# Six of the second branch's gate blocks as seven block products a pair, with closer substitutions and a later chain for the new tokens

## The chip, the cores and the metric

The kernel runs on one core of a Trainium2 chip. The metric is the device time of one execution in microseconds (us). About 0.5% of it, 6 us, is what a measurement of this kernel can tell from no change.

The engines are named as the profile names them: PE (TensorE, matmuls), PEld (its weight loads), DVE (VectorE), ACT (ScalarE), POOL (GpSimd) and SP (SyncE, which here issues most DMAs).

## The reference, cut to what matters

One decoder layer works on 512 prompt positions and 8 new tokens, 520 columns in all, with a model width of 1024. A first SwiGLU block, a token mixer and a second SwiGLU block follow each other, each between two RMS norms. The mixer has two branches, retention and gated delta, of four heads each, and merges them by two sigmoid gates of 1024 channels each:

```python
proj = (h @ w_in).astype(f32)
rq, rk, rv, rg, conv_in, gz, ga, gb, gate_r, gate_g = jnp.split(proj, idx, axis=-1)
...
cq, s_conv_new = short_conv(conv_in, s_conv.astype(f32), gdn_conv_w.astype(f32))
gq = gq * lax.rsqrt(jnp.sum(gq * gq, axis=-1, keepdims=True) + EPS) * (GDN_DK ** -0.5)
gk = gk * lax.rsqrt(jnp.sum(gk * gk, axis=-1, keepdims=True) + EPS)
...
a_mat = jnp.eye(c, dtype=jnp.float32) + jnp.where(strict, bc[..., :, None] * dm * kk, 0.0)
u_v = lax.linalg.triangular_solve(a_mat, bc[..., None] * vc, left_side=True, lower=True, unit_diagonal=True)
...
y = (jax.nn.sigmoid(gate_r) * (o_r @ w_ret_branch) + jax.nn.sigmoid(gate_g) * (o_g @ w_gdn_branch))
y = (y @ w_out).astype(h.dtype)
```

The triangular systems have 64 rows, one for each chunk of 64 positions and head. The change bears on `gate_g` (how the product `h @ w_in` is formed for it), on when the triangular systems are solved, and on when the new tokens' part of the delta branch runs. What is computed stays the same.

## The kernel before, in words

All matrices are fp32. To keep the accuracy, an operand is split into a rounded part (`whi`, `xhl`'s first half) and a rest (`wlo`, its second half), and a product is three passes, lines 422 to 424: high by high, low by high, high by low. A unit of weights is a block of 1024 x 128 numbers. It is loaded by SP as `raw` (line 288 for the mixer's input weights), split by ACT (`whi`, line 360) and DVE (`wlo`, line 361), and multiplied with the 520 columns in two halves of 260: 8 contraction blocks x 3 passes x 2 halves = 48 matmuls.

Where two units belong together, the kernel can form them as seven block products instead of eight (the Strassen-Winograd scheme, table `SEVEN`). The two SwiGLU blocks do so for their gate and up weights. A pair then takes 7 x 12 = 84 matmuls in place of 96. For that it needs sums of quarters of the weights: `begin_pair` (line 292) loads three quarters by SP (`s3`, `s1`, `a22`), and `add_sums` (line 305) adds two further quarters to them by DMAs that accumulate, issued by POOL (line 308) six ticks later. `split_seven` (line 363) makes the operands `w` out of them on ACT (line 378) and DVE (line 379), and adds the remaining sums on DVE. It needs factors of the other side too (`T1` to `T4`), made from x by `token_factors` (line 747), and `product7` (line 779) issues the matmuls.

The order of the work is written out by a clock of ticks. `product` calls `tick` (line 224) after each six matmuls. A tick issues what is due among the spawned tasks, which are generators: each yields the number of ticks after which it wants to go on, and the table `LATER` shifts single steps of single tasks. So what stands in each engine's queue is fixed when the program is built, and each engine goes through its queue in order. `prefetch` (line 313) loads and splits units ahead of their use.

The mixer (line 1038) goes through the units of `w_in` in the order of `proj_order`: decay inputs, the delta branch's k, q and v of four heads, the retention branch's q, k and v, then the two output gates of the heads (`RG` and `GZ`), then eight units of the first merge gate (`GR`) and eight of the second (`GG`). After each two merge-gate units stands one unit of branch weights, whose products `br` (48 matmuls for two output blocks) take the heads' outputs `oh` and `ol` as their operands. `branch` (line 1136) merges them on DVE (line 1154) and POOL (line 1155).

With each head's v the task `gdn_head` (line 1376) is spawned. It forms `rr`, the normalisation of q and k, by a small power on POOL (line 1394), and from it `cols` on DVE (line 1403). Then `inverse` (line 1492) inverts the unit triangular matrices `AT`: blocks of 32 are laid out through DRAM (`s1`, then `L`), 31 steps of two POOL instructions each (lines 1521 and 1522, on the tile `pack`) do the substitution, eight DMAs write the result to DRAM (line 1527), four read it back turned (line 1530), DVE transposes it (line 1537), and PE uses it, in `pV` first (line 1547). `TURN` = 48 is the least distance in ticks between two heads' substitutions, and the substitution's own 31 steps are spread over 39 ticks.

With the last v of the delta branch the task `decode_gdn` (line 1711) is spawned for the new tokens. It sends out two states by POOL, convolves on DVE (`dcv`, lines 1722 and 1724), takes a silu on ACT, squares on DVE (`gsq`, line 1728), and PE sums the squares in `cs` (line 1615, in `rsqrt`).

`finish_decode` (line 1769) writes the new tokens' columns into `oh` and `ol`, ahead of the first `br` of each branch; the main loop calls it itself.

## Time and profile before

| | before |
|---|---|
| median of 3 runs | 1226.57 us (1226.17 to 1230.27) |
| the profiled execution's own time | 1229.19 us |
| its span | 1227.4 us |
| mean granted PE clock | 0.983 |
| matmuls | 9921 |
| PE busy | 1192.2 us (97%) |
| DVE busy | 898.7 us (73%) |
| ACT busy | 575.0 us (47%) |
| POOL busy | 278.4 us (23%) |
| moved by DMA | 170.36 MB |

The page gives each engine's busy time, then the chain of work that ended last, then groups of instructions by line. "out<-in" names the tile that an instruction writes and those that it reads; a bracket such as [2.30 <-POOL rr L1394] says how long the engine stood idle before it and what ended that. The lines of a helper stand for all who call it: 422 to 424 are the matmuls of every product. Matmuls overlap, so the duration of one (some 280 ns) is longer than its pitch.

### The profile page before, as it was taken

To read this page: it belongs to the slowest core of one execution; us is meant where nothing else is said; L and a number is where in the kernel's file an instruction comes from. 1 tells how busy PE (TensorE), PEld (TensorE's weight loads), DVE (VectorE), ACT (ScalarE), POOL (GpSimd) and SP (SyncE) were. 2 spreads that over 40 slices of the span, in tenths; PEclk is the share of its full clock that TensorE was granted. 3 is DMA by queue.
4 is the path that set the end of the run, shared out by engine and by line. 5 is a ranking of instruction groups with operands and counts; after the bars stand their busy time and mean duration, and the time that the engine had idled before them with its cause. 6 is when DMAs were issued, how large, how long until landed. Compare 5 with 4: busy or idle time off the path is not lost.

```text
span 1227.4 us, 25453 instructions
## 1 busy us (share of the span) xinstructions
PE 1192.2 (97%) x9921; PEld 1179.4 (96%) x9921; DVE 898.7 (73%) x1932; ACT 575.0 (47%) x1197; POOL 278.4 (23%) x501
## 2 busy tenths in 40 slices
PE   8999999999999998999999999999999999999995
PEld 7999999999998998999999999999999999999994
DVE  8988888776547887767676666547888888867554
ACT  6655666553325664322333343324565666653330
POOL 4211111000014148545541112213311111000003
PEclk8999999999998999999999999999999999999997
DMA  6887776223351433332435454342587777332352
GB/s 195 217 196 193 188 178 159 63 81 95 95 178 60 166 106 95 108 102 83 132 102 166 164 200 138 125 164 69 162 233 189 186 177 187 93 93 80 96 167 70
DMA packets 79688, 170.36 MB, mean 139 GB/s; under 512 B 17232, under 2 KB 20144, under 8 KB 79568
## 3 DMA queue, kind: packets, MB, share of 16 engines
q1 hardware_dynamic: 67280, 144.46, 37.0%
q0 software_dynamic: 12288, 24.29, 11.2%
q8 instruction: 77, 1.26, 0.4%
q14 instruction: 43, 0.35, 0.1%
HBM read 156.88 MB, written 11.83 MB: 137 GB/s over the span
## 4 chain that ended last, share of the span: by engine, by line
PE 79%; DVE 9%; ACT 4%; POOL 2%; issue 2%; DMA 2%; SPq 0%; ACTq 0%; DVEq 0%; POOLq 0%
PE sv L423 10%; PE sv L422 10%; PE sv L424 10%; PE p L422 6%; PE dn L422 6%; PE dn L424 6%; PE dn L423 6%; PE p L423 6%; PE p L424 6%; DVE wlo L361 2%; PE br L422 1%; PE br L423 1%; PE br L424 1%; PE g L423 1%; PE g L424 1%
## 5 line engine op out<-in xcount | busy, mean ns | idle before, releaser
L422 PE MATMUL p<-xhl,whi 128*128 128x260 f32 x768 | 227.7, 296 | 0.0
L424 PE MATMUL p<-xhl,wlo 128*128 128x260 f32 x768 | 218.4, 284 | 1.4 <-DVE wlo L361 1.4
L423 PE MATMUL p<-xhl,whi 128*128 128x260 f32 x768 | 218.9, 285 | 0.0
L361 DVE TENSOR_TENSOR wlo<-raw,whi 128x1024 fp32r<-128x1024 f32 (+2 forms) x120 | 139.6, 1170 | 43.2 <-ACT whi L360 41.5
L422 PE MATMUL sv<-th,w 128*128 128x260 f32 x592 | 167.4, 283 | 0.5 <-ACT q L848 0.5
L423 PE MATMUL sv<-tl,w 128*128 128x260 f32 x592 | 167.7, 283 | 0.0
L424 PE MATMUL sv<-th,w 128*128 128x260 f32 x592 | 167.3, 283 | 0.0
L424 PEld LDWEIGHTS p<-xhl,wlo 128*128 128x128 f32 x768 | 146.7, 191 | 1.6 <-DVE wlo L361 1.6
L422 PEld LDWEIGHTS p<-xhl,whi 128*128 128x128 f32 x768 | 146.7, 191 | 1.0
L423 PEld LDWEIGHTS p<-xhl,whi 128*128 128x128 f32 x768 | 147.0, 191 | 0.0
L379 DVE TENSOR_TENSOR w<-s,w 128x512 fp32r<-128x512 f32 x148 | 101.7, 689 | 38.8 <-ACT w L378 37.7
L308 POOL DMA_DIRECT2D s<-gu_in x74 | 65.1, 977 | 284.8 <-DMA s<-gu_in 143.1
L424 PE MATMUL dn<-hh,wlo 128*128 128x260 f32 x448 | 126.7, 283 | 1.2 <-DVE wlo L361 1.2
L360 ACT CAST whi<-raw 128x1024 fp32r<-128x1024 f32 (+2 forms) x120 | 115.4, 970 | 26.4 <-DMA raw<-dn_in 16.8
L422 PE MATMUL dn<-hh,whi 128*128 128x260 f32 x448 | 126.9, 283 | 0.0
L423 PE MATMUL dn<-hl,whi 128*128 128x260 f32 x448 | 126.6, 282 | 0.0
L423 PE MATMUL sv<-xhl,w 128*128 128x260 f32 x444 | 125.6, 283 | 0.0
L424 PE MATMUL sv<-xhl,w 128*128 128x260 f32 x444 | 125.4, 283 | 0.0
L422 PE MATMUL sv<-xhl,w 128*128 128x260 f32 x444 | 125.3, 282 | 0.0
L422 PEld LDWEIGHTS sv<-th,w 128*128 128x128 f32 x592 | 111.5, 188 | 0.8 <-ACT q L848 0.7
L424 PEld LDWEIGHTS sv<-th,w 128*128 128x128 f32 x592 | 111.7, 189 | 0.0
L423 PEld LDWEIGHTS sv<-tl,w 128*128 128x128 f32 x592 | 111.2, 188 | 0.0
(412 smaller groups left out, 3249.7 us busy)
## 6 DMA issues: line engine op xcount, KB each, us to landing
raw<-gu_in SPq DMA_DIRECT2D x50, 512.0 KB, 5.2
raw<-win_in SPq DMA_DIRECT2D x48, 512.0 KB, 3.7
s<-gu_in SPq DMA_DIRECT2D x74, 256.0 KB, 5.7
s<-gu_in POOLq DMA_DIRECT2D x74, 256.0 KB, 5.2
raw<-dn_in SPq DMA_DIRECT2D x32, 448.0 KB, 3.5
a<-gu_in SPq DMA_DIRECT2D x37, 256.0 KB, 6.1
x<-x SPq DMA_DIRECT2D x32, 260.0 KB, 5.3
raw<-dn_in SPq DMA_DIRECT2D x16, 512.0 KB, 3.7
```

Source lines behind the costliest of these rows:

```text
L308: self.nc.gpsimd.dma_start(out=out, in_=term, accum_op=ALU.add)
L360: self.nc.scalar.copy(hi[:, ks], t[:, ks])
L361: self.nc.vector.tensor_tensor(lo[:, ks], t[:, ks], hi[:, ks].bitcast(F32), ALU.subtract)
L379: nc.vector.tensor_tensor(w[:, 1], t[i], w[:, 0].bitcast(F32), ALU.subtract)
L422: mm(ps, hi[:, k, :], xh, start=first, stop=False, skip_group_check=more)
L423: mm(ps, hi[:, k, :], xl, start=False, stop=False, skip_group_check=more)
L424: mm(ps, lo[:, k, :], xh, start=False, stop=last, skip_group_check=more)
```

## The change

The last six of the eight `GG` units become three pairs of seven products each (`PLAIN_GATES` = 2 units stay plain). `begin_pair` and `load_to` take `win` as a source. The factors `T1` to `T4` are made in a new task, `gate_factors`, which runs beside the `GR` gates: it waits 40 ticks, and then four times reads four pieces of x back from DRAM (260 KB for each two blocks and half) and calls `factors`, which is the body of the old `token_factors`, twice. A new function, `gate_pair`, issues the products and writes the two gates. While `GG` runs, `prefetch` splits at most one unit for each tick (`most`).

The distance between two heads' substitutions goes from 48 to 40 ticks, and a substitution's steps take one more tick at each eighth step and not at each fourth, 35 ticks in all. In `decode_gdn` the wait of 20 ticks at the start becomes 28, and the one of 6 ahead of `cs` gets 2 more. `finish_decode` becomes a task spawned ahead of the `GR` units, with its instructions grouped by engine; the main loop ticks on until it is done.

```diff
-TURN = 48
+TURN = 40
+FACTORS = (40, 10, 6)
...
-    ("decode_gdn", 0): {10: 3},
+    ("decode_gdn", 0): {1: 8, 2: 2, 10: 3},
...
             for i in range(n, n + 2 * KD, 2):
-                out += [("win", i, 0, 8), ("win", i + 1, 0, 8), ("wbr", (i - n) // 2, 0, 8)]
+                if i < n + KD + PLAIN_GATES:
+                    out += [("win", i, 0, 8), ("win", i + 1, 0, 8)]
+                else:
+                    out += [("seven", "win", i, z) for z in GATE_ORDER]
+                out.append(("wbr", (i - n) // 2, 0, 8))
...
+PLAIN_GATES = 2
+GATE_ORDER = (0, 1, 2, 3, 5, 4, 6)
...
-                s1, s3, a22 = self.begun.pop((u[1], m), None) or self.begin_pair(u[1], m)
+                s1, s3, a22 = self.begun.pop(u[1:3], None) or self.begin_pair(u[1], u[2])
...
-            ahead += j > 0 and not seven and self.unit_list[j - 1][0] == "down7"
+            ahead += j > 0 and not seven and self.unit_list[j - 1][0] in ("seven", "down7")
...
+    def gate_factors(self, x_from, xs, gcol, F, first):
+
+        yield FACTORS[0]
+        for k0 in range(0, KH, 2):
+            x = [[self.slot("x", (P, 2, HC)) for _ in range(2)] for _ in range(2)]
+            for z in range(2):
+                for hf in range(2):
+                    k1 = k0 + z * KH
+                    self.nc.sync.dma_start(out=x[z][hf], in_=x_from[:, hf, k1 : k1 + 2])
+            yield FACTORS[1]
+            for k in (k0, k0 + 1):
+                yield from self.factors(k, [x[z][hf][:, k - k0] for z in range(2) for hf in range(2)], xs, gcol, F)
+                yield FACTORS[2]
+        self.begun["win", first] = self.begin_pair("win", first)
...
+        def heads(out):
+            while not ready(out):
+                yield 0
+            yield from self.finish_decode(out)
+            done.add(out)
+
+        self.spawn(heads(RG))
+        self.spawn(heads(GZ))
...
-                project(g, m)
-                project(g, m + 1)
-                if m == 0:
-                    while any((out, h) not in self.oparts for h in range(H)) or out not in self.dec_done:
-                        self.tick()
-                    self.finish_decode(out)
-                    ox = [[self.ohl[out, h, hf] for h in range(H)] for hf in range(2)]
+                if g == GR or m < PLAIN_GATES:
+                    project(g, m)
+                    project(g, m + 1)
+                else:
+                    gate[g, m], gate[g, m + 1] = self.gate_pair(F, r, first + m - PLAIN_GATES + 2 if m + 2 < KD else None, None)
+                while out not in done:
+                    self.tick()
+                ox = [[self.ohl[out, h, hf] for h in range(H)] for hf in range(2)]
...
+    def gate_pair(self, F, r, after, between):
...
+        if after is not None:
+            self.begun["win", after] = self.begin_pair("win", after)
+        for i in GATE_ORDER:
+            self.product7(SEVEN, F, "sv", banks, i)
+            a, b, c = banks
+            if i in (0, 1, 2, 5):
+                v[i] = self.work("q" if i == 1 else "u", HC)
+                nc.scalar.copy(v[i], c if i == 1 else a)
...
+            if i in (3, 4, 5):
+                t = self.work("t", HC)
+                x, y, op = ((c, 2, ALU.subtract), (b, 0, ALU.add), (v.get(1), 5, ALU.subtract))[i - 3]
+                tt(t, x, v[y], op)
+                scaled(*((1, 0), (0, 0), (1, 1))[i - 3], t)
...
-            yield 1 + (j % 4 == 0)
+            yield 1 + (j % 8 == 0)
```

How this moves the queues is seen at three places. The first is POOL's queue at the end of head 0's substitution (the tile `pack`; `rr` is the normalisation that head 3's `cols` wait for, `L` the triangular blocks). Before:

```order
L1521 TENSOR_TENSOR pack_5880<-L_5877,pack_5880 128x4x3
L1522 TENSOR_TENSOR pack_5880<-pack_5880 128x4x3
L1394 TENSOR_TENSOR rr_6538<-se_6536,mhalf 128x8
L1304 COPY rdec<-rp_6540 128x8
L1521 TENSOR_TENSOR pack_5880<-L_5877,pack_5880 128x4x2
L1522 TENSOR_TENSOR pack_5880<-pack_5880 128x4x2
L1521 TENSOR_TENSOR pack_5880<-L_5877,pack_5880 128x4
L1522 TENSOR_TENSOR pack_5880<-pack_5880 128x4
```

In the changed kernel the same place reads:

```order
L1612 TENSOR_TENSOR pack_5880<-L_5877,pack_5880 128x4x3
L1613 TENSOR_TENSOR pack_5880<-pack_5880 128x4x3
L1612 TENSOR_TENSOR pack_5880<-L_5877,pack_5880 128x4x2
L1613 TENSOR_TENSOR pack_5880<-pack_5880 128x4x2
L1612 TENSOR_TENSOR pack_5880<-L_5877,pack_5880 128x4
L1613 TENSOR_TENSOR pack_5880<-pack_5880 128x4
L1623 MEMSET TT_6547 128x512
L1626 MEMSET pack_1107_6549 64x256
L1485 TENSOR_TENSOR rr_6559<-se_6557,mhalf 128x8
L1395 COPY rdec<-rp_6561 128x8
L1612 TENSOR_TENSOR pack_6390<-L_6386,pack_6390 128x31
```

The `rr` and the `rdec` behind it have moved from within the substitution to behind its last step, ahead of head 1's first.

The second place is PE's queue where the new tokens' sums (`cs`) and head 0's first use of its inverse (`pV`) stand among the projections `p`. Before, `cs` is the 3789th matmul:

```order
L423 MATMUL p_6659<-xhl_5181,whi_6416 128x260
L424 MATMUL p_6659<-xhl_5181,wlo_6417 128x260
L1615 MATMUL cs_6679<-ones,gsq_6628 64x1
L422 MATMUL p_6658<-xhl_5040,whi_6416 128x260
L423 MATMUL p_6658<-xhl_5040,whi_6416 128x260
```

Some 80 matmuls further on, as the 3869th, comes `pV` (a row with x4 holds four matmuls):

```order
L423 MATMUL p_6752<-xhl_5232,whi_6552 128x260
L424 MATMUL p_6752<-xhl_5232,wlo_6553 128x260
L1547 MATMUL pV_6825<-pack_5880,AT_5805 32x32 x4
L1547 MATMUL pV_6826<-pack_5880,AT_5805 32x32 x4
L422 MATMUL p_6751<-xhl_5070,whi_6552 128x260
```

In the changed kernel `pV` comes first, as the 3835th matmul, and head 2's `gbc` stands right behind it:

```order
L436 MATMUL p_6757<-xhl_5168,whi_6573 128x260
L437 MATMUL p_6757<-xhl_5168,wlo_6574 128x260
L1638 MATMUL pV_6773<-pack_5880,AT_5805 32x32 x4
L1638 MATMUL pV_6774<-pack_5880,AT_5805 32x32 x4
L1339 MATMUL gbc_6793<-cst,gg 128x128 x4
L435 MATMUL p_6756<-xhl_5009,whi_6573 128x260
```

And `cs` comes behind it, as the 3869th:

```order
L436 MATMUL p_6757<-xhl_5207,whi_6573 128x260
L437 MATMUL p_6757<-xhl_5207,wlo_6574 128x260
L1706 MATMUL cs_6841<-ones,gsq_6706 64x1
L1260 MATMUL tr_6848<-cst,rv_6643 128x128 x4
L435 MATMUL p_6756<-xhl_5062,whi_6573 128x260
```

The two have changed places: `pV` has moved 34 matmuls ahead and `cs` 80 back.

The third place is POOL's queue where the `GG` gates begin (`srets_out` and `sgdns_out` are the new tokens' states, `t` is the merging of a branch's output; the number behind a name tells its buffers apart). Before:

```order
L1654 DMA srets_out<-sd_1631_9767 128x512
L1654 DMA sgdns_out<-sd_1641_9864 128x512
L1654 DMA srets_out<-sd_1656_9945 128x512
L1155 TENSOR_TENSOR t_1689_10186<-t_1689_10186,yr_1535_9163 128x260
L1155 TENSOR_TENSOR t_1690_10189<-t_1690_10189,yr_1535_9163 128x260
```

In the changed kernel the accumulating loads of the pairs (`s3`, `s1`) stand among them:

```order
L1745 DMA srets_out<-sd_1658_9831 128x512
L321 DMA s3_1688_9992<-win_in 128x512
L321 DMA s1_1687_9991<-win_in 128x512
L1745 DMA sgdns_out<-sd_1660_9858 128x512
L321 DMA s3_1711_10106<-win_in 128x512
L321 DMA s1_1710_10105<-win_in 128x512
L1745 DMA srets_out<-sd_1700_10054 128x512
L1745 DMA sgdns_out<-sd_1703_10086 128x512
L1246 TENSOR_TENSOR t_1738_10307<-t_1738_10307,yr_1552_9225 128x260
L1246 TENSOR_TENSOR t_1739_10310<-t_1739_10310,yr_1552_9225 128x260
L321 DMA s3_1731_10266<-win_in 128x512
L321 DMA s1_1730_10265<-win_in 128x512
```

Each pair is begun twice, once when `load_to` reaches it and once when `gate_factors` or `gate_pair` asks for it: `split_seven` reads `s3_1688` and `s3_1731`, while `s3_1711`, `s1_1710` and their like are loaded by SP and summed by POOL a second time and read by nobody. With the second pair's first begin the loads stand behind the merging of a branch (`t`).

More of the change, by code (lines that the diff above doesn't have):

```diff
@@ L209, in __init__ @@
         self.ahead = 0
+        self.most = 9
         self.tasks = []
@@ L311, in cost, with prefetch @@
         return 1 if self.unit_list[j][0] in ("seven", "down7", "wab") else 2
-    def prefetch(self, force=False, most=9):
+    def prefetch(self, force=False, most=None):
         if self.hold and not force:
@@ L317, in prefetch @@
         free = SPLIT_BUFS + sum(1 for t in self.freed if force or t + 2 <= self.now)
-        last = self.split_next + most
+        last = self.split_next + (most or self.most)
         while self.split_next < min(last, len(self.unit_list)):
@@ new lines, in token_factors @@
+        for k in range(KH):
+            yield from self.factors(k, [self.x_of(z, hf) for z in (k, k + KH) for hf in range(2)], xs, gcol, F)
+    def gate_factors(self, x_from, xs, gcol, F, first):
[11 more added lines that the diff above has]
+        self.begun["win", first] = self.begin_pair("win", first)
```

105 lines of the change are left out of this document (71 added, 34 removed).

## Prediction

> **What bounds the kernel now.** I read the page first, for the engine that is never free and for the chain of work that ended last.
>
> ```profile
> PE 1192.2 (97%) x9921; PEld 1179.4 (96%) x9921; DVE 898.7 (73%) x1932; ACT 575.0 (47%) x1197; POOL 278.4 (23%) x501
> PE 79%; DVE 9%; ACT 4%; POOL 2%; issue 2%; DMA 2%; SPq 0%; ACTq 0%; DVEq 0%; POOLq 0%
> ```
>
> TensorE is busy for 97% of the span and is 79% of the chain. A matmul removed is therefore worth its pitch, not its duration, and anything else counts only where it makes TensorE wait. Both are seen in the busy time by stretches of 25 us (columns: TensorE, weight loads, VectorE, ScalarE, GpSimd, granted clock, DMA share, GB/s).
>
> ```profile
> 75.00:100.00 25.00, 25.00 (x211) 25.00 (x210) 20.84 (x42) 14.45 (x30) 4.06 (x5) 1.00 0.82 179
> 475.00:500.00 25.00, 19.27 (x143) 18.84 (x142) 16.74 (x47) 5.61 (x20) 16.56 (x37) 0.86 0.38 99
> 875.00:900.00 25.00, 23.64 (x198) 23.01 (x197) 21.72 (x43) 15.20 (x28) 5.23 (x5) 1.00 0.95 275
> 900.00:925.00 25.00, 24.48 (x202) 24.18 (x201) 22.34 (x46) 14.86 (x33) 5.27 (x6) 1.00 0.79 196
> ```
>
> A full stretch holds 211 matmuls of 260 columns: 25/211 = 0.1185 us each. The stretch at 475 us holds 143; the missing 68 are 8.1 us. It is the largest hole inside the mixer, and the view of TensorE's waits names it:
>
> ```profile
> PE cs L1615 <- DVE gsq L1728: 5.7, 1, 5.7
> PE br L422 <- ACT oh L1776: 1.1, 2, 0.5
> ```
>
> The timelines of VectorE, GpSimd and TensorE show how that wait came about.
>
> ```profile
> 484.87 0.16 DVE L1403 TENSOR_TENSOR cols<-se,rr 128x4 f32<-128x4 f32 x1 [2.30 <-POOL rr L1394]
> 487.81 0.23 DVE L1728 TENSOR_TENSOR gsq<-dcv 128x64 f32<-128x64 f32 x1 [0.35 <-ACT dcv L1725]
> 449.42 0.55 POOL L1521 TENSOR_TENSOR pack<-L,pack 128x31 f32<-128x31 f32 x1 [1.63 <-DMA L<-s]
> 475.88 1.12 POOL L1304 COPY rdec<-rp 128x8 f32<-128x8 f32 x1 [1.33 <-DVE rp L1303]
> 483.19 1.65 POOL L1394 TENSOR_TENSOR rr<-se,mhalf 128x8 f32<-128x8 f32 x1
> 484.80 0.18 POOL L1304 COPY rdec<-rp 128x8 f32<-128x8 f32 x1
> 485.80 0.26 POOL L1522 TENSOR_TENSOR pack<-pack 128x4 f32<-128x4 f32 x1
> 482.08 0.28 PE L424 MATMUL p<-xhl,wlo 128*128 128x260 f32 x1
> 488.09 0.37 PE L1615 MATMUL cs<-ones,gsq 128*64 128x1 f32 x2 [5.73 <-DVE gsq L1728]
> ```
>
> GpSimd works off head 0's substitution (pack, L1521 and L1522) from 449.42 to 486.06, 36.6 us. The small `rr` stands in that queue; VectorE waits for it, the new tokens' convolution (dcv, gsq) stands behind that on VectorE, and TensorE stands before `cs` from 482.2 to 488.1: 5.9 us. The rest of the 8.1 us, 2.2 us, is the half-rate clock after it, as stretches of 5 us show:
>
> ```profile
> 370.00:375.00 5.00, 3.75 (x26) 2.93 (x26) 4.11 (x11) 2.73 (x6) 3.57 (x4) 0.82 0.00 0
> 375.00:380.00 5.00, 5.00 (x24) 4.92 (x25) 4.01 (x6) 5.00 (x15) 2.14 (x3) 0.50 0.52 161
> 485.00:490.00 5.00, 1.91 (x9) 1.90 (x10) 4.37 (x17) 1.22 (x2) 4.45 (x9) 0.59 0.47 140
> 490.00:495.00 5.00, 5.00 (x32) 4.79 (x30) 0.03 (x1) 1.62 (x2) 2.47 (x10) 0.73 0.14 22
> ```
>
> **The change part by part.** *Seven block products.* Each of three gate pairs takes 84 matmuls instead of 96: 36 x 0.1185 = **-4.3 us**, since TensorE is the bound there.
>
> *finish_decode as a task.* One of the two waits of `br` for `oh` goes, the second branch's, which now finds its operands 200 matmuls early: **-0.5 us**. The first keeps its place: 16 matmuls ahead of it instead of 17.
>
> *New tokens later.* `cs` moves from the 3789th matmul to the 3869th, 80 x 0.1185 = 9.5 us later. Its wait was 5.9 us, so it and its clock loss go: **-8.1 us**. What is late next is head 0's substitution itself.
>
> *Substitutions closer.* With four ticks fewer and other small matmuls ahead, head 0's first use of the inverse, `pV`, moves from the 3869th to the 3835th matmul. Without the wait at `cs` TensorE is there at 482.2 + 46 x 0.1185 = 487.7. The result is not. In before it went through DRAM like this:
>
> ```profile
> 486.09 4.99 SPq L1527 DMA_DIRECT2D s<-pack  x8
> 492.49 1.73 SPq L1530 DMA_DIRECT2D pack<-s  x4
> DMA to landing us min/median/max: 1.6/1.7/1.8
> 500.40 0.31 DVE L1537 STREAM_TRANSPOSE pack<-pack 128x128 f32<-128x128 f32 x1
> L1522 POOL TENSOR_TENSOR pack<-pack 128x30 f32<-128x30 f32 (+23 forms) x35 | 13.1, 374 | 2.7
> L1521 POOL TENSOR_TENSOR pack<-L,pack 128x30 f32<-128x30 f32 (+23 forms) x35 | 12.1, 345 | 3.8 <-DMA L<-s 1.6
> ```
>
> From the last step (486.06) over eight writes, four reads (the last issued at 493.8) and 1.7 us to landing it is 495.5, so 9.4 us, and 0.31 for the transpose. In before nobody saw this: TensorE, held back by `cs`, came to `pV` only after 500. In the changed order one `rr` (1.65) and one `rdec` (0.18) stand behind the substitution and not in it: its end is 484.2. The wait of 1.33 for `rp` may go too, since that copy stands six rows later: 482.9. I take 483.5, so `pV` can start at 493.2 and TensorE waits 5.5 us; with the same 2.2 us of half clock **+7.7 us**. Bounds: nothing comes off GpSimd's queue, 486.06 + 9.7 - 487.7 = 8.1, with the clock 10.3; the other end is below. Heads 1 to 3 come 94 to 181 matmuls earlier too. Head 1's substitution follows head 0's on GpSimd: 483.5 + 36.6 + 9.7 = 530, and its `pV`, 348 matmuls behind head 0's, is reached at 493.2 + 41.2 + 2.2 = 536.6. The next two stand 405 and 294 matmuls further on, 48 and 35 us against 36.6 of substitution, so at least 7 us of room stays: zero, and where GpSimd is later by more than that, the excess.
>
> Of the clock the Trainium skill says ("TensorE: Matmul & The Clock Gate", Part 1) that half rate follows an idle window of about 3.4 us. By that a wait under 3.4 us would cost its length alone and this term would end at 3.4 and not 5.6. This trace differs: the stretch at 375 ran 24 matmuls at 0.50 though the stretch before it lost only 1.25 us of busy time.
>
> *Operands of the seven products.* What a pair adds goes beside TensorE, if there is room. The prices:
>
> ```profile
> L361 DVE TENSOR_TENSOR wlo<-raw,whi 128x1024 fp32r<-128x1024 f32 (+2 forms) x120 | 139.6, 1170 | 43.2 <-ACT whi L360 41.5
> L379 DVE TENSOR_TENSOR w<-s,w 128x512 fp32r<-128x512 f32 x148 | 101.7, 689 | 38.8 <-ACT w L378 37.7
> q1 hardware_dynamic: 67280, 144.46, 37.0%
> q0 software_dynamic: 12288, 24.29, 11.2%
> s<-gu_in SPq DMA_DIRECT2D x74, 256.0 KB, 5.7
> s<-gu_in POOLq DMA_DIRECT2D x74, 256.0 KB, 5.2
> L308 POOL DMA_DIRECT2D s<-gu_in x74 | 65.1, 977 | 284.8 <-DMA s<-gu_in 143.1 <-DVE w L379 59.6 <-ACT w L378 25.3
> L378 ACT CAST w<-s 128x512 fp32r<-128x512 f32 x148 | 91.2, 618 | 34.5 <-DVE s L374 23.3 <-PE sv L424 7.6 <-DVE s L382 3.3
> L845 ACT COPY u<-sv 128x260 f32<-128x260 f32 x37 | 13.9, 376 | 12.1 <-PE sv L424 10.4
> L1155 POOL TENSOR_TENSOR t<-t,yr 128x260 f32<-128x260 f32 x16 | 14.2, 905 | 28.1 <-DVE t L1154 28.1
> L1154 DVE SCALAR_TENSOR_TENSOR t<-gate,br 128x260 f32<-128x260 f32 x16 | 6.1, 420 | 1.9 <-PE br L424 1.9
> 775.00:800.00 25.00, 25.00 (x212) 25.00 (x211) 14.13 (x26) 7.79 (x12) 6.41 (x7) 1.00 0.34 112
> 700.00:725.00 25.00, 25.00 (x213) 25.00 (x212) 16.39 (x41) 9.81 (x21) 2.16 (x4) 1.00 0.63 212
> ```
>
> VectorE: 27 half-size steps (21 splits, six sums) x 0.689 - 6 x 1.17 = 11.6 us over the 396 matmuls (47 us) of the three pairs, 6.2 per 25 us: 14.13 becomes 20.3 of 25, and nine more evictions at 0.42 bring it to 22. DMA: the order shows each pair begun twice, and the tiles of the second begin are read by nobody. So 18 loads of 256 KB, ten state reads of that size and seven of 512 KB on the SP queue make 11.0 MB, and 12 accumulating loads and six state writes on GpSimd's 4.7 MB, in 54 us. By the queues' shares a megabyte takes 0.370 x 1227.4/144.46 = 3.14 us and 0.112 x 1227.4/24.29 = 5.66 us: 34.5 + 26.6 = 61 us, a full DMA. The nearest rows are the 50 us from 875, VectorE at 22 and DMA at 0.95 and 0.79: 13 + 9 matmuls short, **+2.6 us** in 50. I take that. Room is scarce at one place: a pair's accumulating load is issued once the branch before it has left GpSimd (0.42 + 2 x 0.905 after `br`, issue 0.98, landing 5.2), and a cast of it (0.62) stands on ScalarE ahead of a copy (0.38) that a product 96 matmuls behind that `br` (11.4 us) waits for: 9.4 us, so 2.0 of room. Bounds: 0 (the row at 75: VectorE 20.84, DMA 0.82, nothing lost), and 10.3 (below).
>
> *Factors.* Eight reads of 260 KB, 16 VectorE steps of 260 columns at 0.42 and eight of double size at 0.69 make 12.2 us in the 43 us of the first branch's gates, 7.1 per 25 beside the 16.39 of the row at 700: under 25. Zero; without that cover the same 1.3 us per 25, some 2 us.
>
> Sum: -4.3 - 0.5 - 8.1 + 7.7 + 2.6 = -2.6. The profiled execution took 1229.19 us (span 1227.4, 1.8 outside it), 2.6 above the median of 1226.57. The terms are differences, so I take them from the median: **1224.0 us**.
>
> **The rivals.** *The hole closes.* If the substitution ends by 478, `pV` never waits. For it: steps of one kind took 0.19 to 1.10 us there, and 70 of them at 0.21 to 0.25, the short kind, would be 9 us less than the 25.2 measured. Against it: the long ones lie all through. It gives 1224.0 - 7.7 = 1216.3.
>
> *The gate stage goes over to DMA* (slower than before). If 61 us of transfers must pass in 54, TensorE loses 7.1. The last pair's accumulating load then lands after 10.4 us and not 5.2, past its 2.0 of room by 3.2: 10.3 in place of 2.6, 1231.7. It decides from 5.2 us on, where the gains are used up. For it: 0.95 already cost 13 matmuls. Against: queues hold reserves, and the unread copies delay only what stands behind them. The Trainium skill ("DMA: Bandwidth & Descriptors", Issuing engines are not separate DMA queues) has transfers of all issuers share the same 16 engines and interleave. By this rule the unread loads on SP do slow GpSimd's.
>
> *Fewer matmuls, no time.* If VectorE sets the pairs' pace, the change does not do what it says and the 4.3 us come back: 1228.3. For it: 22 of 25 us; against it: 20.84 held nothing up.
>
> **How the numbers follow.** Forecast 0.42, hole closes 0.32, DMA 0.15, no time 0.11. A measurement can tell about 0.5% from no change, 6.1 us. Faster than 1220.4: nearly all of the second case (0.30) and a fifth of the forecast's (0.08). Slower than 1232.7: half of the DMA case and small tails of the others, 0.14. The range goes from the closing hole with a free gate stage (1216.3 - 2.6 = 1213.7) to the DMA case, rounded up (1232.0). The forecast's own is 1219 to 1227.
>
> **What would show it.** Right: no wait at `cs`; TensorE's longest wait is `pV` for the transposes, 5 to 6 us at about 488, a clock of about 0.5 behind it; GpSimd's last substitution step at 483 to 484; in the gate stage DMA near 0.95 and waits under 1.5 us. Wrong: `pV` without a wait; a pair's copies on ScalarE waiting for accumulating loads for over 3 us; later heads' `pV` waiting; the split of a gate's weights on VectorE as the releaser.

## The result, and the profile after

| | before | after |
|---|---|---|
| median of 7 runs each | 1228.26 us (1226.17 to 1230.27) | 1237.05 us (1232.98 to 1238.49) |
| ratio after/before, 95% interval | | 1.0076 [1.0064, 1.0087] |
| the profiled execution's own time, span | 1229.19, 1227.4 us | 1237.59, 1235.6 us |
| matmuls | 9921 | 9885 |

The kernel became slower by 0.76%. The forecast of 1224.0 was wrong in sign, and the result lies outside its range. (In what follows one execution of `e9_once_late2` and one of `e12_mid_late2`, far off the others at 1376 and 4813 us, are left out.)

The page's engine line, its chain and its two DMA queues answer to those shown of before.

```profile
PE 1191.7 (96%) x9885; PEld 1178.4 (95%) x9885; DVE 926.9 (75%) x1986; ACT 591.1 (48%) x1240; POOL 282.3 (23%) x513
PE 75%; DVE 10%; ACT 4%; issue 4%; POOL 4%; DMA 2%; SPq 1%; ACTq 0%; POOLq 0%; DVEq 0%
q1 hardware_dynamic: 70592, 149.73, 37.5%
q0 software_dynamic: 14016, 27.44, 12.7%
```

The matmuls went down by 36, as the change says, but TensorE's busy time hardly did (1191.7 against 1192.2), and its share of the chain fell from 79% to 75%: the span now holds more time in which TensorE waits. The view of its waits says for what:

```profile
PE sv L435 <- ACT u L1212: 9.2, 4, 6.7
PE pV L1638 <- DVE pack L1628: 5.0, 1, 5.0
PE pX L1664 <- DVE pack L1660: 2.5, 1, 2.5
PE br L435 <- DVE yr L1235: 1.2, 1, 1.2
```

The wait at `cs` (5.7) is gone and `pV` for the transposes has come, as forecast. The first row was not forecast: `sv` are the block products of the gate pairs, and they wait for ScalarE's copies `u` of the results of earlier products (line 1212). The busy time by stretches shows where (columns as before: TensorE, weight loads, VectorE, ScalarE, GpSimd, clock, DMA share, GB/s):

```profile
475.00:500.00 25.00, 20.04 (x161) 19.48 (x160) 16.45 (x44) 7.37 (x14) 19.91 (x56) 0.86 0.41 118
750.00:775.00 25.00, 18.29 (x137) 18.08 (x136) 17.91 (x42) 11.13 (x25) 8.20 (x11) 0.86 0.83 215
775.00:800.00 25.00, 22.56 (x172) 21.93 (x170) 20.49 (x43) 13.21 (x30) 10.57 (x14) 0.93 0.69 179
```

Up to the delta branch's gates nothing is won and nothing lost: the fifth `br`, the first product behind the two plain gate units, begins at 741.70 in after and at 741.81 in before. From there to the first matmul of the second SwiGLU block it takes 115.68 us (to 857.38) in after and 105.39 (to 847.20) in before: **+10.3 us**, where the prediction had -1.7 (seven products -4.3, their operands +2.6). The stretch at 750 alone holds 137 matmuls. This is how it comes about, in after's timelines of ScalarE, VectorE, GpSimd and TensorE (start, duration, then the instruction):

```profile
734.13 0.62 ACT L391 CAST w<-raw 128x512 fp32r<-128x512 f32 x1 [1.62 <-DMA raw<-win_in]
744.25 0.62 ACT L391 CAST w<-s 128x512 fp32r<-128x512 f32 x1 [9.50 <-DMA s<-win_in]
757.28 0.42 ACT L1251 ACTIVATE yh<-t 128x260 fp32r<-128x260 f32 x1 [2.88 <-POOL t L1246]
758.28 0.36 ACT L1212 COPY u<-sv 128x260 f32<-128x260 f32 x1
...
744.91 0.69 DVE L392 TENSOR_TENSOR w<-s,w 128x512 fp32r<-128x512 f32 x1 [9.12 <-ACT w L391]
755.54 0.75 DVE L1245 SCALAR_TENSOR_TENSOR t<-gate,br 128x260 f32<-128x260 f32 x2
...
733.43 1.85 POOL L321 DMA_DIRECT2D s<-win_in  x2
756.50 1.43 POOL L1246 TENSOR_TENSOR t<-t,yr 128x260 f32<-128x260 f32 x2
...
758.69 0.58 PE L435 MATMUL sv<-th,w 128*128 128x260 f32 x1 [6.71 <-ACT u L1212]
```

The first pair's two accumulating loads are issued from 733.43 on, and the cast of the quarter that the first of them completes, `w<-s`, is ScalarE's next instruction but one. It can start only at 744.25, 10.8 us behind the issue, when the load has landed. ScalarE stood 9.50 us before it, VectorE 9.12 behind ScalarE. The products themselves did not need that quarter so early: the second product, which reads it, begins at 750.39. But everything behind the cast was now late: the pair's other splits, gates, and state updates of the same queues, behind them the merging of the fifth branch (`t` on VectorE at 755.54, on GpSimd at 756.50, `yh` on ScalarE at 757.28), and only behind `yh` the copy `u` at 758.28. The third product adds to the result buffer (`banks`) that this copy has to read first, so TensorE stood 6.7 us, from 752.0 to 758.7; from 756.2 to 763.0 it was at half clock.

The DMA was full meanwhile. After in stretches of 5 us:

```profile
735.00:740.00 5.00, 5.00 (x44) 5.00 (x43) 0.79 (x2) 0.00 (x0) 0.85 (x2) 1.00 0.89 274
740.00:745.00 5.00, 4.75 (x40) 4.54 (x38) 0.09 (x1) 0.62 (x1) 0.00 (x0) 1.00 1.07 320
```

VectorE 0.79 and 0.09 of 5 us, ScalarE 0.00 and 0.62: two engines with work queued, both idle, beside a TensorE that still ran on what had been prepared. The bill came when TensorE ran dry at 752.0, 7.8 us after the load had landed.

### The profile page after: what moved, and what is told of

Its sections match the earlier page's. It is cut to its first block, busy times and chain, and to the rows that moved or that the text cites. A ratio compares the mean times of both kernels' runs of the same rounds, so it can differ in the third digit from the quotient of the medians.

```text
span 1235.6 us, 25561 instructions
## 1 busy us (share of the span) xinstructions
PE 1191.7 (96%) x9885; PEld 1178.4 (95%) x9885; DVE 926.9 (75%) x1986; ACT 591.1 (48%) x1240; POOL 282.3 (23%) x513
## 4 chain that ended last, share of the span: by engine, by line
PE 75%; DVE 10%; ACT 4%; issue 4%; POOL 4%; DMA 2%; SPq 1%; ACTq 0%; POOLq 0%; DVEq 0%
PE sv L435 10%; PE sv L437 10%; PE sv L436 10%; PE dn L437 6%; PE dn L435 6%; PE dn L436 6%; PE p L435 4%; PE p L437 4%; PE p L436 4%; DVE wlo L374 1%; PE g L436 1%; PE g L435 1%; PE g L437 1%; ACT whi L373 1%; PE sp L1764 1%
## 5 line engine op out<-in xcount | busy, mean ns | idle before, releaser
L435 PE MATMUL p<-xhl,whi 128*128 128x260 f32 x672 | 199.0, 296 | 0.0
L435 PE MATMUL sv<-th,w 128*128 128x260 f32 x640 | 182.9, 286 | 9.7 <-ACT u L1212 9.2
L437 PE MATMUL p<-xhl,wlo 128*128 128x260 f32 x672 | 190.0, 283 | 1.8 <-DVE wlo L374 1.8
L436 PE MATMUL p<-xhl,whi 128*128 128x260 f32 x672 | 190.0, 283 | 0.0
L436 PE MATMUL sv<-tl,w 128*128 128x260 f32 x640 | 182.3, 285 | 0.0
L437 PE MATMUL sv<-th,w 128*128 128x260 f32 x640 | 182.2, 285 | 0.0
L392 DVE TENSOR_TENSOR w<-s,w 128x512 fp32r<-128x512 f32 x160 | 110.0, 689 | 51.1 <-ACT w L391 49.0
L435 PE MATMUL sv<-xhl,w 128*128 128x260 f32 x480 | 135.7, 283 | 0.0
L437 PE MATMUL sv<-xhl,w 128*128 128x260 f32 x480 | 135.4, 282 | 0.0
L436 PE MATMUL sv<-xhl,w 128*128 128x260 f32 x480 | 135.4, 282 | 0.0
L435 PEld LDWEIGHTS sv<-th,w 128*128 128x128 f32 x640 | 122.1, 191 | 10.8 <-ACT u L1212 10.0
L437 PEld LDWEIGHTS p<-xhl,wlo 128*128 128x128 f32 x672 | 126.8, 189 | 2.3 <-DVE wlo L374 2.3
L435 PEld LDWEIGHTS p<-xhl,whi 128*128 128x128 f32 x672 | 127.1, 189 | 0.9
L391 ACT CAST w<-s 128x512 fp32r<-128x512 f32 x160 | 98.7, 618 | 60.3 <-DVE s L387 32.3
L436 PEld LDWEIGHTS p<-xhl,whi 128*128 128x128 f32 x672 | 127.2, 189 | 0.0
L437 PEld LDWEIGHTS sv<-th,w 128*128 128x128 f32 x640 | 122.1, 191 | 0.0
```

The source lines that it names most:

```text
L391: nc.scalar.copy(w[:, 0], t[i])
L392: nc.vector.tensor_tensor(w[:, 1], t[i], w[:, 0].bitcast(F32), ALU.subtract)
L435: mm(ps, hi[:, k, :], xh, start=first, stop=False, skip_group_check=more)
L436: mm(ps, hi[:, k, :], xl, start=False, stop=False, skip_group_check=more)
L437: mm(ps, lo[:, k, :], xh, start=False, stop=last, skip_group_check=more)
```

## The experiments

**The theory:** the loss comes from the place of one cast in ScalarE's queue. It stands 24 matmuls (2.8 us) of program behind the issue of the load that it waits for, and in-order queues carry its wait to everything behind it. **The rivals:** the second begin of each pair, whose copies nobody reads, fills the DMA; the stage as such has too much VectorE or DMA work (the DMA rival of the prediction), wherever the casts stand; or the loss belongs to the earlier part, to the closer substitutions. Each ratio below is to `before` timed beside the kernel, with its 95% interval. The medians of `before` itself lay between 1226.17 and 1228.26, so kernels are compared by these ratios.

**e1_once: each pair begun once.** The two early begins are taken out, so that the begin in `load_to` remains.

```diff
-        self.begun["win", first] = self.begin_pair("win", first)
...
-        if after is not None:
-            self.begun["win", after] = self.begin_pair("win", after)
```

> Each pair is begun once (by load_to alone): nine loads of 256 KB and six accumulating loads that nobody reads are gone, everything else stays. Theory 'unread copies': ScalarE's 9.5 us before the cast of the first pair's summed quarter are transfers that stand behind too many others; with a third of them gone that wait falls below 5 us, TensorE's 6.7 us at the third product falls below 2, and the time is 1227 to 1230 us. Theory 'begun too late': the accumulating load is issued only some 3 us of work ahead of the cast, full DMA or not; the wait stays above 6 us and the time at 1233 to 1237. Rival 'VectorE sets the pace': its work is the same, so 1236 to 1238, and VectorE stays above 95% between 745 and 755.

Measured: 1233.51 us, 1.0053 [1.0038, 1.0069]. The stage took 115.35 us, as in after (115.68). ScalarE's timeline, the waits and the stretches of 5 us, each of e1:

```profile
741.90 0.62 ACT L391 CAST w<-s 128x512 fp32r<-128x512 f32 x1 [7.37 <-DMA s<-win_in]
```

```profile
PE sv L435 <- ACT u L1209: 9.2, 4, 6.7
PE pV L1635 <- DVE pack L1625: 2.6, 1, 2.6
```

```profile
735.00:740.00 5.00, 5.00 (x44) 5.00 (x44) 0.26 (x1) 0.00 (x0) 0.00 (x0) 1.00 1.05 333
740.00:745.00 5.00, 4.49 (x38) 4.29 (x37) 1.67 (x4) 0.62 (x1) 0.00 (x0) 1.00 1.02 332
```

With nine loads and six accumulating ones fewer the DMA is as full, the first pair's accumulating loads land 10.0 and 12.3 us after their issue (10.7 and 12.2 in after), the cast still stands 7.37 us and the products wait as long to a tenth. The unread copies do not make the loss. By the ratios e1 is 0.23%, 2.8 us, below after, but not in this stage. Of the 5.0 us between the two profiled spans (1230.6 and 1235.6) 1.6 lie ahead of the fifth `br` (740.08; `pV` waits 2.6 us in place of 5.0, without half clock behind it), 0.3 in the stage, and 3.1 behind it, where at 861 us after runs 6.8 us at half clock and e1 3.4.

**e2_front: the change without its pairs.** All eight units stay plain; substitutions, new tokens and `finish_decode` are as in after.

```diff
-PLAIN_GATES = 2
+PLAIN_GATES = 8
...
-            self.most = 1 if g == GG else 9
-            if g == GR:
-                self.spawn(self.gate_factors(x_from, xs, V_MPRE, F, first))
```

> No pairs: all eight units of the second gate are formed as before, and no factors are made; the closer substitutions, the later chain of the new tokens and finish_decode as a task stay. Theory 'the loss is in the pairs': the first half is neutral (the wait at cs gone, one of 5 us at pV and one of 2.5 us at pX in its place), so 1226 to 1230, the same as before. Rival 'the first half costs': 1232 or more, with waits at pV and pX that no saved wait pays for. If half the clock losses of the changed kernel come from the first half, 1224 or 1232 by turns.

Measured: 1227.08 us, 1.0000 [0.9990, 1.0011]. The waits of e2:

```profile
PE pV L1635 <- DVE pack L1625: 4.8, 1, 4.8
PE pX L1661 <- DVE pack L1657: 2.4, 1, 2.4
```

So all the rest of the change is neutral: `cs` is replaced by `pV` and a second wait, `pX`. The whole loss is that of the pairs and their factors. The stage takes 104.69 us here. In after it has 36 matmuls (4.3 us) less and takes 11.0 more, so what the pairs' operands cost is **15.3 us**.

**e3_gates: the pairs alone.** The substitutions and the new tokens go back to their places of before.

```diff
-TURN = 40
+TURN = 48
...
-    ("decode_gdn", 0): {1: 8, 2: 2, 10: 3},
+    ("decode_gdn", 0): {10: 3},
...
-            yield 1 + (j % 8 == 0)
+            yield 1 + (j % 4 == 0)
```

> The pairs alone: TURN 48, substitution steps over 39 ticks and the new tokens' chain as before; factors, pairs and finish_decode as changed. Theory 'the loss is in the pairs': 1235 to 1239, the wait at cs of 5.9 us back, none at pV, and the same waits of TensorE in the second gate as in the changed kernel. Rival 'the first half costs': 1229 to 1232.

Measured: 1239.33 us, 1.0096 [1.0078, 1.0114]: no better than after, but with other waits than the expectation had. The waits of e3, then its timelines of ScalarE and TensorE:

```profile
PE tr L1260 <- DVE go L1580: 7.4, 1, 7.4
PE pS L1556 <- DVE AT L1553: 5.7, 2, 4.2
PE sv L435 <- ACT u L1212: 3.3, 4, 1.5
```

```profile
741.46 0.62 ACT L391 CAST w<-s 128x512 fp32r<-128x512 f32 x1 [5.90 <-DMA s<-win_in]
746.75 1.11 PE L1260 MATMUL tr<-cst,go 128*128 128x128 f32 x4 [7.45 <-DVE go L1580]
```

With the old distance the last heads' work falls into the first branch's gates, where the factors are now made. The long wait at `tr` is the same cast again: ScalarE stands 5.90 us for the first pair's load, VectorE 5.82 behind it, and what stands behind them on VectorE this time is a head's `go`, which TensorE needs for `tr`. So the loss is taken ahead of the fifth `br` (753.11), and from there e3 takes only 105.2 us, to 858.34. Ahead of the wait at `pS` ScalarE stood 8.13 us for the x reads of the factors. The closer substitutions win nothing by themselves (e2), and without them the late load costs as much.

**e5_latecast: the same first load, the cast later in the queue.** The pairs' units are split at most two units ahead of their use and no longer eight. The first pair's begins and loads stay where after has them; of the later pairs the second begin goes with the shift.

```diff
+            if self.unit_list[j][:2] == ("seven", "win"):
+                ahead = 2
```

> The changed kernel with its double begins, but the split of a pair's weights is issued at most two products ahead and not eight. Theory 'order of ScalarE's queue': the first pair's summed quarter landed at 744.2, before its product could start (749), so only the cast's early place made ScalarE and VectorE idle for 9 us; the 6.7 us wait falls below 2 us and the time to 1228 to 1231. Rival 'the transfers are late': the products themselves then wait for them, the loss keeps its size, 1235 or more. A third possibility: splits two products ahead are too near to their use, and several waits of about 1 us for casts take the place of the long one, 1231 to 1234.

Measured: 1227.49 us, 1.0016 [1.0003, 1.0029]: by the ratios 0.60%, 7.4 us, below after. ScalarE's timeline, the waits and a stretch of e5:

```profile
737.86 0.63 ACT L1800 ACTIVATE sd<-sd 128x512 f32<-128x512 f32 x1 [2.15 <-DMA sd<-sret_in]
742.46 0.62 ACT L393 CAST w<-s 128x512 fp32r<-128x512 f32 x1 [2.09 <-DMA s<-win_in]
```

```profile
PE sv L437 <- ACT u L1214: 2.7, 4, 1.0
```

```profile
740.00:745.00 5.00, 5.00 (x44) 5.00 (x43) 2.68 (x8) 1.53 (x4) 0.39 (x1) 1.00 1.07 337
```

The DMA is as full as in after (1.07), and the accumulating load lands hardly earlier against its issue (9.5 us, 732.97 to 742.46), but ScalarE does other work in between and stands 2.09 us before the cast instead of 9.50. With the waits for other loads just ahead (3.02 and 2.15 in e5, 1.62 in after) it is 7.3 us against 11.1; what goes ahead of the cast in e5 are gates and state updates. The stage falls to 107.9 us. This is the separation wanted: with a landing almost as late, most of the loss goes when the casts are put elsewhere in ScalarE's queue. The shift is of all three pairs' casts; what the first one alone is worth was not separated. In program order 108 matmuls instead of 24 now lie between the load's issue and its reader.

**e4_early and e6_mid: the load earlier.** The cast stays, and each pair is begun once, a pair sooner than in after: pair one at the start of `gate_factors` in e4 (below), with the last x read (`if k0 == KH - 2`, inside the loop) in e6.

```diff
         yield FACTORS[0]
+        self.begun["win", first] = self.begin_pair("win", first)
         for k0 in range(0, KH, 2):
...
-        self.begun["win", first] = self.begin_pair("win", first)
...
+            if g == GG:
+                self.begun["win", first + 2] = self.begin_pair("win", first + 2)
...
-                    gate[g, m], gate[g, m + 1] = self.gate_pair(F, r, first + m - PLAIN_GATES + 2 if m + 2 < KD else None, None)
+                    gate[g, m], gate[g, m + 1] = self.gate_pair(F, r, first + m - PLAIN_GATES + 4 if m + 4 < KD else None, None)
```

> Each pair is begun once, and earlier: the first at the start of the factors' task, the second with the first plain unit of the second gate, the third with the first pair's products. Theory 'begun too late': ScalarE's waits for accumulating loads before the casts of the pairs go (below 1 us), TensorE loses under 2 us in the second gate, and the time is 1222 to 1226, some 4 us under before. Theory 'unread copies' expects no more than the run that begins each pair once. Rival 'VectorE sets the pace': ScalarE's waits go, but TensorE waits for splits and copies all the same, 1232 or more.

> As the run with early begins, but the first pair is begun with the last round of x reads, and not ahead of the first. Theory 'begun too late': that run's new wait of 3.3 us at pS came from x reads standing behind the pair's loads, and ScalarE's 5.9 us before xd with them; it goes, the casts still find their sums, and the time falls from 1229 to 1224 to 1226. Rival 'VectorE sets the pace of the stage': the wait moves and the time stays at 1228 to 1230.

Measured: e4 1229.28 us, 1.0013 [1.0000, 1.0027], stage 103.94; e6 1229.89 us, 1.0030 [1.0017, 1.0043], stage 110.9. Both are above what was expected of them. In e4 no cast of a pair waits for an accumulating load any more and the stage is the shortest but one of the study (e8: 103.6), but the x reads for the factors now stand behind the pair's loads on SP, and the time goes elsewhere: e4's timeline of ScalarE and its waits.

```profile
699.77 0.51 ACT L793 ACTIVATE xd<-x,vec 128x260 f32<-128x260 f32 x1 [5.89 <-DMA x<-x]
```

```profile
PE pS L1558 <- DVE AT L1555: 3.3, 1, 3.3
PE sv L435 <- ACT u L1214: 2.4, 3, 1.5
```

e6 begins the pair behind the x reads. The `pS` wait goes, and another cause makes the products wait: VectorE's splits now come in one block ahead of the branch's merging, and `yh` is late though no accumulating load is. In e6's waits and timeline of ScalarE:

```profile
PE sv L435 <- ACT u L1215: 6.0, 3, 3.8
```

```profile
750.89 0.42 ACT L1254 ACTIVATE yh<-t 128x260 fp32r<-128x260 f32 x1 [2.91 <-POOL t L1249]
```

So the late load was one way to make `yh` and the copies behind it late; early splits are another. A third stands beside them: at 729.0 in e6 ScalarE and VectorE had stood 5.0 and 4.6 us before the factors' `xd`, which by the profile a transfer of a state to DRAM (`srets_out<-sd`) released. That `xd` waited there for the buffer of `sd` is likely, but not shown. e12 (below) differs from e6 by the splits alone, still has 3.6 and 3.2 us of that wait, and is 0.35% faster.

**e7_yh and e8_pv: two repairs on top of e6.** e7 lets the merging's last steps (`yh`, `yl`) go two ticks later, so that the copies no longer stand behind them. e8 also lets head 0's inverse be used five ticks later, against the wait at `pV`.

```diff
-SLOTS = 68
+SLOTS = 67
...
+    **{("branch", n): {2: 2} for n in range(10, 16)},
...
-        bufs = {"t": 2, "s": 2, "u": 3, "v": 1, "q": 2, "c": 1}.get(tag, 1)
+        bufs = {"t": 4, "s": 2, "u": 3, "v": 1, "q": 2, "c": 1}.get(tag, 1)
...
+        self.first_inverse = True
...
-        yield 16
+        self.first_inverse, late = False, 5 if self.first_inverse else 0
+        yield 16 + late
```

> As e6_mid, and the two activations yh of the second gate's last six blocks come two ticks later (with four buffers for t and one big buffer less). Theory 'order of ScalarE's queue': the waits that are left in the pairs (1.5, 0.6 and below, of sv for the copies u) are copies that stand behind yh, and yh behind VectorE's and GpSimd's merging; they fall below 0.5 us in sum, 1 to 2.5 us less than e6_mid. Rival 'VectorE sets the pace': no difference beyond 0.5 us.

> As e7_yh, and head 0's pV comes five ticks later. Theory: the substitution's way through DRAM ends at about 491, TensorE now comes there at 491.5 and not at 486: no wait at pV and none of the half clock behind it, 3 to 6 us less than e7_yh, 1217 to 1221. Rival: the wait goes on to pP and pX, which wait for VectorE's copies, and the time stays within 1 us of e7_yh.

Measured: e7 1227.47 us, 1.0009 [0.9996, 1.0022]; e8 1226.56 us, 1.0007 [0.9992, 1.0022]. In e7 the waits of `sv` for `u` fell from 6.0 to 2.7 us (below 0.5 was expected). In e8 `pV` waits as long as ever, and its row names another instruction of VectorE:

```profile
PE pV L1644 <- DVE gdm L1714: 5.1, 1, 5.1
```

VectorE comes to this place late, since one of its splits ahead of it waited 2.42 us for ScalarE, whose own cast had waited 4.40 us for the unit's load. The shift of the one step does not close the hole here.

**e9, e10, e11, e12: where the cast stands, dosed.** e9 and e10 are e1 with the pairs split at most two and four units ahead; e11 and e12 are e6 with four and two. The edit is that of e5, with 2 or 4.

> Each pair begun once, and its splits issued at most two products ahead: the two corrections of e1_once and e5_latecast together. Theory 'order of the queue, and the unread copies cost nothing of their own once ScalarE does not stand before the cast': within 1.5 us of e5_latecast, 1226 to 1229. Rival 'the unread copies cost': 1222 to 1225, the waits of 0.5 to 1.3 us in the pairs of e5_latecast gone.

> As e9_once_late2 with splits at most four products ahead. If two are too near to their use, the small waits for casts go and this is 1 to 3 us under e9_once_late2, 1222 to 1226, under before for the first time; if ScalarE again comes to the cast of a summed quarter ahead of its transfer, a wait of over 2 us for it is back and the time is 1229 to 1233.

> As e6_mid with splits at most four products ahead. Its accumulating loads land long before the casts, so ScalarE has no reason to stand; e6_mid's wait of 3.8 us (yh behind VectorE, which works off the splits first) shrinks below 2 and the time is 1223 to 1226. Rival 'VectorE sets the pace': the splits come later but are as many, 1227 to 1230 as e6_mid.

> As e6_mid (each pair begun once and early), with the splits at most two products ahead as in e5_latecast: 226, 192 and 180 matmuls between an accumulating load and the cast that reads it, in place of 24, 60 and 60 in the changed kernel. Theory 'distance from the accumulating load to the cast': no cast waits for a transfer, ScalarE and VectorE come to the merging of the branch in time, 1223 to 1227, at the time of before or a little under. Rival 'VectorE sets the pace': 1229 to 1231 as e6_mid and e11_mid_late4.

The table sets the times beside the number of matmuls that the program has between the issue of each pair's accumulating load and the first cast that reads it.

| kernel | matmuls between, pairs 1/2/3 | median us | ratio to before |
|---|---|---|---|
| e10_once_late4 | 24 / 0 / 0 | 1246.05 | 1.0155 [1.0132, 1.0178] |
| after | 24 / 60 / 60 | 1237.05 | 1.0076 [1.0064, 1.0087] |
| e9_once_late2 | 108 / 0 / 0 | 1234.81 | 1.0062 [1.0045, 1.0079] |
| e1_once | 24 / 60 / 60 | 1233.51 | 1.0053 [1.0038, 1.0069] |
| e11_mid_late4 | 142 / 168 / 156 | 1231.05 | 1.0032 [1.0018, 1.0046] |
| e6_mid | 142 / 168 / 156 | 1229.89 | 1.0030 [1.0017, 1.0043] |
| e5_latecast | 108 / 48 / 48 | 1227.49 | 1.0016 [1.0003, 1.0029] |
| e4_early | 315 / 168 / 156 | 1229.28 | 1.0013 [1.0000, 1.0027] |
| e12_mid_late2 | 226 / 192 / 180 | 1226.27 | 0.9995 [0.9984, 1.0007] |

In e9 and e10 the later split makes the only begin that is left later too, so they shift the load as well as the cast: not the clean test of the cast's place that was meant, but a dose of the distance. The times expected of e9, e10 and e11 were all too low; that of e12 came. Where nothing is left for two pairs, the wait is found there: in e10 a cast of the second pair stands over 10 us.

```profile
772.02 0.62 ACT L393 CAST w<-s 128x512 fp32r<-128x512 f32 x1 [10.61 <-DMA s<-win_in]
```

The table is in the order of the ratios. Among the kernels with at least 48 matmuls for every pair and 108 for the first, the distance no longer orders the times; that the work around the merging does is argued from e6 and e11 against e12. e12 is the best of the pairs and level with before, no more. What became of its 4.3 us is seen in one stretch of 105 us in e12, then in e2:

```profile
745.00:850.00 105.00, 101.85 (x832) 99.88 (x831) 73.43 (x143) 45.76 (x91) 23.68 (x29) 1.00 0.49 150
```

```profile
745.00:850.00 105.00, 103.77 (x865) 103.23 (x863) 60.45 (x113) 37.38 (x68) 22.26 (x27) 1.00 0.40 130
```

VectorE has 13.0 us more work in e12 and is at 73.43 of 105, not full; yet TensorE gets through 33 matmuls fewer in the same time (3.9 us at 0.1185). The stage takes 106.1 us against 104.7: 4.3 saved, 5.7 given back in waits of TensorE of 1.0 us or less, of which the view names `sv` for `u` (2.4 us in four); the rest is not accounted for. In the stage alone e4 and e8 are 0.7 and 1.1 us under e2, but they lose that and more ahead of it.

## Why the prediction was wrong, point by point

- **Seven products, -4.3.** The 36 matmuls are gone. The gain is not seen in any kernel as a whole: e12, with every load in time, gives it back.
- **finish_decode, -0.5; new tokens, -8.1.** Right in kind: no wait at `cs`, none of `br` for `oh` among the longer ones.
- **pV, +7.7.** Right, step by step, but for the wait behind it. GpSimd's last step of head 0's substitution and the four reads that bring the result back, in after, with the waiting `pV` and the `pX` that follows:

```profile
481.12 0.21 POOL L1613 TENSOR_TENSOR pack<-pack 128x4 f32<-128x4 f32 x1
487.82 1.74 SPq L1621 DMA_DIRECT2D pack<-s  x4
491.28 0.87 PE L1638 MATMUL pV<-pack,AT 32*32 32x32 f32 x16 [4.96 <-DVE pack L1628]
512.79 0.68 PE L1664 MATMUL pX<-TT,pack 64*64 64x64 f32 x8 [2.53 <-DVE pack L1660]
```

  The end was 481.3 for the 483.5 forecast, TensorE there at 486.3 for 487.7, the wait 5.0 for 5.5, and 6.8 us of half clock from 489.9 on. That the wait came out so near is luck: two errors cancelled. Not foreseen was `pX`, 2.5 us and 3.4 of half clock (1.7 us lost), in the same head's substitution: I had followed the first use of the inverse and not the one behind it. With it the part up to the gates comes to about -0.9 + 4.2 = +3.3 by the terms; measured were -0.1 to the fifth `br` and a ratio of 1.0000 for e2. Part of what made up for these 3 us is seen in the clock: before runs at half clock from 373.25 for 6.83 us and from 560.98 for 3.41, after at neither place. Over the first of them, from the 2800th matmul to the 3200th, after is 1.3 us faster, though TensorE's queue is the same there in both. The "hole closes" rival did not come; it would have needed the end at 478.
- **Operands of the seven products, +2.6: the step that failed.** Measured 15.3. The step compared totals over the stage (VectorE at 22 of 25 us, DMA at 0.95) with the nearest stretches, and looked for scarce room at one place only, the loads of the second and third pair, with 2.0 us. The pair that decided was the first: by an estimate from after's trace its 6.7 us of wait and 6.8 us at half clock make some 10 of the 15.3. Its load is issued by `load_to` from within `prefetch`, and `prefetch`, allowed eight units ahead, puts the cast 24 matmuls behind the accumulating part. These 2.8 us against the row of 5.2 us to landing would have shown the wait even without a full DMA, and the order of ScalarE's queue was there to be read; I read only GpSimd's and TensorE's. The upper bound of 10.3 was too low for the same reason: to the excess of the transfers (7.1) it added the wait of one copy (3.2), where the wait of an in-order queue goes to all that stands behind.
- **The DMA rival (slower, 0.15)** was nearest. Its landing of 10.4 us was seen (10.7), with a DMA at 1.07; its place, the last pair, and its price were not. And it decided by the landing, where e5 shows that the landing alone does not decide: with a DMA as full the cost is small if the readers stand later. The unread copies, to which the prediction gave part of the traffic, do not matter to the stage (e1). Of the Trainium skill's rule that transfers of all issuers interleave on the same engines ("DMA: Bandwidth & Descriptors", Issuing engines are not separate DMA queues) the trace agrees: GpSimd's two loads took 10.7 and 12.2 us while SP's transfers filled the same stretch. What the prediction drew from it, that the unread loads slow GpSimd's, is not seen: without them these loads took 10.0 and 12.3 us (e1).
- **Fewer matmuls, no time (0.11).** Not by VectorE as bound, which stays at 73.43 of 105 us even in e12; but its outcome, a pair that saves nothing, is where the repaired kernels arrive.
- **Factors, 0.** Right in after's setting: the fifth `br` begins at 741.70 with them and at 741.32 without (e2). In e3, without the closer substitutions, `pS` waits behind them.

With 15.3 in place of 2.6 the sum becomes +10.1; the profiled executions differ by 8.4. The rest of the kernel behind the stage ran 2.0 us shorter (1235.6 - 857.38 = 378.2 against 1227.4 - 847.20 = 380.2). Behind the stage after loses time at 861 us, at half clock, and makes up for it at the very end of the kernel, where the change does nothing: before is at half clock for its last 14.5 us, after for 8.4. What of e1's gain over after is owed to its edit, and why the accumulating loads took 9.5 to 10.8 us here and not 5.2, beyond the full DMA beside them, stays open.

## What to carry to other kernels

A load that is issued early is worth nothing if its reader stands close behind it in an in-order queue: count the program between the issue and the first instruction that reads it, in units of the bound engine's time, and compare that with the landing time under a full DMA. Price such a wait by all that stands behind it on that engine, not by the reader alone. And a transformation that saves 4% of a stage's matmuls and adds a quarter to a third to the instructions of the engines beside them (VectorE 143 for 113, ScalarE 91 for 68) can lose its gain in many small late hand-overs; the best layout tried here brought it to zero.

## What the runs showed of the hardware

The half clock comes on a fixed grid of time. Measured in steps of 0.2 us, ten traces (before, after, e1, e2, e4 to e8, e12) hold 41 stretches of half clock between 360 and 900 us. Each begins a whole number of 3.413 us after the first of its trace, to 0.01 or less of such a step, and lasts 3.41 or 6.83 us (in e3 and e10 one stretch each lasts 10.24). In after they begin at 489.92, 513.81, 756.16, 780.05 and 861.97: 0, 7, 78, 85 and 109 steps. So the same wait costs its length alone, or up to 3.4 us more, by where it falls in the grid. e12 and then e1, in stretches of 1 us, at the same place of the program:

```profile
488.00:489.00 1.00, 0.00 (x0) 0.00 (x0) 0.00 (x0) 0.00 (x0) 0.77 (x4) 1.00 0.25 38
489.00:490.00 1.00, 0.10 (x2) 0.10 (x3) 0.47 (x2) 0.00 (x0) 1.00 (x3) 0.62 0.46 56
491.00:492.00 1.00, 1.00 (x6) 1.00 (x6) 0.95 (x4) 0.00 (x0) 0.81 (x3) 0.50 1.08 381
```

```profile
488.00:489.00 1.00, 0.00 (x0) 0.00 (x0) 0.00 (x0) 0.00 (x0) 0.76 (x4) 1.00 0.23 35
489.00:490.00 1.00, 0.06 (x2) 0.07 (x3) 0.43 (x2) 0.00 (x0) 1.00 (x3) 1.00 0.68 71
491.00:492.00 1.00, 1.00 (x11) 1.00 (x10) 0.95 (x4) 0.00 (x0) 0.84 (x3) 1.00 1.06 385
```

Both wait 2.6 to 2.7 us for `pV`. In e12 a step of the grid begins at 489.24, and 2.0 us of the idle time lie in the one before it: half clock, 11 matmuls a microsecond become 6. In e1 a step begins at 488.76 (20 steps behind its stretch at 420.49), which cuts the wait into 1.4 and 1.2 us: full clock. `pX` of e1 has 2.0 us of its wait in one step and is followed by half clock too. In these ten traces, between 360 and 900 us, every step with over 1.8 us of idle time is followed by half clock. Below that there is no sharp border: of two steps with 1.8 us the one in e7 (from 488.69) is followed by it, the one in e4 (from 485.75) is not.

Idle time is not all of it either. Ten of the 41 stretches follow a step in which TensorE is busy throughout by the profile (at about 420 in seven traces, at 560.98 in before, at 557.50 and 608.70 in e12), and that at 373 in before follows one with 1.3 us idle. What starts these is not explained. One of them, in e6:

```profile
416.80:420.21 3.41, 3.41 (x30) 3.31 (x29) 2.17 (x6) 3.41 (x9) 0.19 (x1) 1.00 1.05 402
420.21:423.62 3.41, 3.41 (x18) 3.41 (x18) 3.20 (x7) 2.45 (x16) 1.69 (x3) 0.50 0.52 151
```

The Trainium skill ("TensorE: Matmul & The Clock Gate", Part 1) has the chip watch a free-running window of about 3.4 us; the grid agrees with that. The reading that the prediction weighed, that a wait under 3.4 us costs only its own length, does not hold in these traces. That the grid's position against the program is what makes executions of one kernel differ by some 3 us is only argued.
